# Between output and up projection: activation sums emitted ahead of the early products, weight splits strewn among them

## The chip, the cores and the metric

The kernel runs on one core of one Trainium2 chip. The metric is device time in microseconds (us) of one execution, the median of several runs. Five engines work side by side, each through its own list of instructions in order: TensorE (PE; its weight loads are listed as PEld), VectorE (DVE), ScalarE (ACT), GpSimd (POOL) and SyncE (SP, which issues nearly all transfers here). They meet through semaphores: an instruction waits until another engine has counted far enough, and everything behind it on its own engine waits with it.

## The reference, cut to what matters

An encoder block on 1024 tokens of width 1024, all in float32: a mixing sub-layer (latent attention and a matrix-memory branch, merged by gates), then an MLP with a squared ReLU, then a last norm. The change stands where the mixing sub-layer's output projection ends and the MLP begins:

```
merged = (jax.nn.sigmoid(gate_a) * (y_attn @ w_branch_mla[l])
          + jax.nn.sigmoid(gate_b) * (y_mlstm @ w_branch_mlstm[l]))
x = x + merged @ w_out[l]                                # output projection, 1024 x 1024
u = rmsnorm(x, norm_mlp_g[l]) @ w_mlp_up[l]              # up projection, 1024 x 4096
x = x + jnp.square(jax.nn.relu(u)) @ w_mlp_down[l]       # down projection, 4096 x 1024
```

The norm's factor per token is a positive number, so it goes through the squared ReLU as its square: the kernel leaves it out of the up projection and multiplies it in behind the down projection (`rsq`).

## The kernel before, in words

**Split numbers.** Every float32 operand of a matmul is split into a high part (`h`, rounded to the fp32r type by a cast on ACT, L79) and a low part (`l`, what the cast left, by a subtraction on DVE, L80). A product is then three matmuls: high by high, high by low, low by high. `split` is thus always ACT first, DVE second, and a product can start when the cast is done but needs the subtraction by its second or third matmul.

**Output projection** (the loop at L1193). Eight token tiles of 128 in two halves of four. Each tile takes 48 matmuls into a PSUM tile of two banks (`a`, two such tiles), then DVE adds the residual (L1202, `xm`), and SP stores the sum for the end of the kernel (L1204). Once a half is there, PE transposes it (L1215) into single-bank PSUM tiles (`b`, four of them, handed round) and ACT copies each with the norm's gain to SBUF (L1216, `xf`): four blocks for the half, `blk[K half, token half, i]`. For the first half they are split at once. ACT then takes the sums of squares of the four `xm` tiles (L1225, `msq`).

**Up projection.** It is worked by pairs of 128-column weight blocks, 16 pairs (`Pair`, `up_pair`). With K and the tokens cut in two halves each, a pair is a 2 x 2 by 2 x 2 block product, and it is done with seven block products in place of eight (Winograd's form of Strassen's method). So sums of blocks are needed beforehand:

- of the activations, once for all pairs: T1, T2, T3, T4 (differences of blocks, L1236, `xt`) and block 22, each two tiles of 128x1024, each split (`bh`, `bl`);
- of the weights, for each pair: `sums` (L1109 to L1123) makes S1 to S4 and block 22 with four DVE sums, three casts and three subtractions; `plain` (L1103) only splits the pair's first block.

A product is 4 slices of K by 3 matmuls: 12 matmuls of 128x512 (L1139). Two of the seven products (blocks 11 and 12 by activations of the first token half) need no sums. For the first five pairs (`EARLY`) they are done ahead, by `first_products`: 12 matmuls into a `b` bank, an ACT copy to `r` (L1149), 12 more matmuls into the same bank, a second ACT copy (L1151). The second 12 must wait for the first copy, since they add to the same bank.

**What sets the order.** The kernel's code is written in Python and recorded; a scheduler then lays out each engine's list, mostly in the order in which the code is written, with some exchange of neighbours. Tiles come from pools handed out in turn: 46 slots of 4 KB for nearly everything, four buffers (`wr`) for raw weights. Who takes a slot or a buffer waits until its earlier holder was last read. Before, the order was: both halves with their squares; five times `plain` and `first_products`; `sums` of pair 0; then all the differences and splits T2, T3, T1, T4, 22; then the pairs, each with the `sums` of the next pair ahead of it.

Of the kernel before, what the change touches and what calls it, by code (L numbers as in the profile page):

```python
# [10 lines left out]
F32 = mybir.dt.float32  # L11
F32R = mybir.dt.float32r
I32 = mybir.dt.int32
AF = mybir.ActivationFunctionType
ALU = mybir.AluOpType
# [3 lines left out]
P = 128  # L19
# [4 lines left out]
EPS = 1e-6  # L24
# [14 lines left out]
def kernel(ctx: ExitStack, tc: tile.TileContext, x, positions, norm_mix_g, w_in, mla_q_norm_g,  # L39
                      mla_w_uq, mla_kv_norm_g, mla_w_ukv, mlstm_conv_w, mlstm_conv_b, mlstm_igate_b,  # L40
                      mlstm_fgate_b, mlstm_out_norm_g, w_branch_mla, w_branch_mlstm, w_out, norm_mlp_g,
                      w_mlp_up, w_mlp_down, norm_final_g, out, dbg=None):
    nc = tc.nc
# [12 lines left out]
    def nm(p):  # L56
        cnt[0] += 1
        return f"{p}{cnt[0]}"

    def slot(shape, dt=F32, p="s"):  # L60
        return sl.tile(shape, dt, tag="s", name=nm(p))
# [4 lines left out]
    def bankA(p="a"):  # L66
        return psa.tile([P, 1024], F32, tag="A", name=nm(p))

    def bankB(p="b"):
        return psb.tile([P, 512], F32, tag="B", name=nm(p))  # L70

    def dump(name, ap, dst):
        if name in dbg:
            nc.sync.dma_start(out=dst(dbg[name]), in_=ap)


    def split(h, l, src, scale=None, eng=None):
        if scale is None:
            nc.scalar.copy(out=h, in_=src)  # L79
            (eng or nc.vector).tensor_tensor(out=l, in0=src, in1=h.bitcast(F32), op=ALU.subtract)  # L80
        else:
            nc.scalar.activation(out=h, in_=src, func=AF.Copy, scale=scale)
            nc.vector.scalar_tensor_tensor(out=l, in0=src, scalar=scale, in1=h.bitcast(F32),
                                           op0=ALU.mult, op1=ALU.subtract)
# [113 lines left out]
    def nat_mm(ps, tr, t, wts, extra=()):  # L198

        n = len(wts)  # L200
        for k in range(n):
            xh, xl = tr.tile(t, k)
            wh, wl = wts[k]
            nc.tensor.matmul(out=ps, lhsT=xh, rhs=wh, start=(k == 0), stop=False)  # L204
            nc.tensor.matmul(out=ps, lhsT=xh, rhs=wl, start=False, stop=False)  # L205
            nc.tensor.matmul(out=ps, lhsT=xl, rhs=wh, start=False, stop=(k == n - 1))  # L206
# [84 lines left out]
    for d in range(2):  # L291
        t = tri[d]
# [48 lines left out]
    def vec(n, i):  # L341
        return vecs[:, vo[n] + i:vo[n] + i + 1]
# [783 lines left out]
    pairs = [Pair(p) for p in range(NP)]  # L1126
    EARLY = 5
# [4 lines left out]
    def product(o, p, a, b, first):  # L1132

        ah, al = pairs[p].ops[a]
        for k in range(4):
            bh, bl = B[b][k // 2]
            bh, bl = bh[:, k % 2], bl[:, k % 2]
            for i, (x_, y_) in enumerate(((ah, bh), (ah, bl), (al, bh))):
                nc.tensor.matmul(out=o, lhsT=x_[:, k], rhs=y_, start=(first and k == 0 and i == 0),  # L1139
                                 stop=(k == 3 and i == 2), skip_group_check=True)  # L1140

    early = {}

    def first_products(p):

        b1 = bankB()
        r = slot([P, 2, 512], F32, "r")
        product(b1, p, "11", "11", True)
        nc.scalar.copy(out=r[:, 1], in_=b1)  # L1149
        product(b1, p, "12", "21", False)  # L1150
        nc.scalar.copy(out=r[:, 0], in_=b1)  # L1151
        return r
# [37 lines left out]
    msq = const.tile([P, 8], F32, name="msq")  # L1190
    rsq = const.tile([P, 8], F32, name="rsq")
    blk = {}
    for half in range(2):  # L1193
        xs = []
        for j in range(4):
            t = half * 4 + j
            xx = slot([P, 1024], F32, "xm")
            nc.sync.dma_start(out=xx, in_=x[0, t * P:(t + 1) * P, :])
            pa = bankA()
            for n in range(2):  # L1200
                nat_mm(pa[:, n * 512:(n + 1) * 512], mg, t, wo[n])
            nc.vector.tensor_tensor(out=xx, in0=pa, in1=xx, op=ALU.add)  # L1202
            dump("xmid", xx, lambda o, t=t: o[t])
            nc.sync.dma_start(out=xmd[t], in_=xx)  # L1204
            xs.append(xx)
        if half == 1:
            pairs[0].load(1)
            pairs[0].plain()
        for q in range(4):
            f = slot([P, 2, 512], F32, "xf")  # L1210
            for i in range(2):
                k = 2 * q + i
                pb = bankB()
                for j in range(4):
                    nc.tensor.transpose(out=pb[:, j * P:(j + 1) * P], in_=xs[j][:, k * P:(k + 1) * P], identity=ident)  # L1215
                nc.scalar.activation(out=f[:, i], in_=pb, func=AF.Copy, scale=vec("gmlp", k))  # L1216
            blk[q // 2, half, q % 2] = f
            if half == 0:
                h, l = slot([P, 2, 512], F32R, "bh"), slot([P, 2, 512], F32R, "bl")
                split(h, l, f)  # L1220
                B.setdefault(f"{q // 2 + 1}1", []).append((h, l))
        for j in range(4):
            t = half * 4 + j
            junk = slot([P, 1024], F32, "j")
            nc.scalar.activation(out=junk, in_=xs[j], func=AF.Square, scale=1.0 / 32.0, accum_out=msq[:, t:t + 1])  # L1225
    nc.vector.tensor_scalar(out=rsq, in0=msq, scalar1=EPS, scalar2=None, op0=ALU.add)
    nc.vector.reciprocal(out=rsq, in_=rsq)

    def parts(name, f):
        h, l = slot([P, 2, 512], F32R, "bh"), slot([P, 2, 512], F32R, "bl")  # L1230
        split(h, l, f)
        B.setdefault(name, []).append((h, l))

    def minus(a, b):
        o = slot([P, 2, 512], F32, "xt")
        nc.vector.tensor_tensor(out=o, in0=a, in1=b, op=ALU.subtract)  # L1236
        return o

    for p in range(EARLY):
        if p > 0:  # L1240
            pairs[p].load(1)
            pairs[p].plain()
        early[p] = first_products(p)
    pairs[0].load()
    pairs[0].sums()
    t1 = [minus(blk[0, 1, q], blk[0, 0, q]) for q in range(2)]
    t2 = [minus(blk[1, 1, q], t1[q]) for q in range(2)]
    for q in range(2):
        parts("T2", t2[q])
    for q in range(2):  # L1250
        parts("T3", minus(blk[1, 1, q], blk[0, 1, q]))
    for q in range(2):
        parts("T1", t1[q])
    for q in range(2):
        parts("T4", minus(blk[1, 0, q], t2[q]))
    for q in range(2):
        parts("22", blk[1, 1, q])


    for p in range(NP):  # L1260
# [102 lines left out]
```

## Time and profile before

| | us |
|---|---|
| median of 3 runs | 1719.27 (1718.85 to 1720.53) |
| the profiled execution, its own time | 1718.16 |
| its span, first to last instruction | 1716.5 |
| PE busy, share of the span | 1658.3, 97% |
| DVE, ACT, POOL busy | 927.4, 683.9, 188.2 |
| mean granted TensorE clock | 0.989 of full speed |

The span's times count from its first instruction; a time such as "at 1001.58" below is on that scale. The profile cuts the span in 40 slices of 42.9 us. In 36 of them PE is busy nine tenths or more; the first has 7 and the last 8 tenths, and two in the middle, slices 24 and 25, have 8 and 5: that is the stretch from 987 to 1073 us, between the output projection and the pairs. Slice 25 is also the only one in which the granted clock reads less than 9 tenths: 7. A PE matmul's time in the trace is 0.39 us, but at full clock one starts every 0.23 us; PE's busy time therefore says whether it has work, and the distance of starts says how fast it goes. ACT and DVE overlap the end of one instruction with the start of the next in the same way, by about 0.1 us.

### The profile page before, as it was taken

What the parts mean: (1) busy time and instruction counts of PE and PEld (TensorE: products, weight loads), DVE (VectorE), ACT (ScalarE), POOL (GpSimd) and SP (SyncE); (2) the same over time, 40 slices, a digit from 0 to 9 for tenths busy, and PEclk for the clock granted to TensorE, in tenths of its full rate; (3) what the DMA queues carried; (4) which work ended last, traced back from release to release, by engine and by line L of the source; (5) the groups of instructions that cost most, each with busy time, mean ns of one, the idle gap of its engine ahead of it and who ended that gap; (6) DMA issues with size and microseconds to landing.
All of it is one profiled execution on the core that took longest, in us unless ns stands there. A gap on an engine that the chain in (4) does not pass through costs nothing.

```text
span 1716.5 us, 21981 instructions
## 1 busy us (share of the span) xinstructions
PE 1658.3 (97%) x8613; PEld 1394.4 (81%) x8613; DVE 927.4 (54%) x1405; ACT 683.9 (40%) x1211; POOL 188.2 (11%) x363
## 2 busy tenths in 40 slices
PE   7999999999999999999999985999999999999998
PEld 6789989888879979898878863778888788888886
DVE  5676766632233386777873217655444564444324
ACT  6254443531122476766732333445443531111101
POOL 4112020100002434343200000000000000000001
PEclk9999999999999999999999997999999999999999
DMA  7112110113221000000165211443332673332002
GB/s 212 37 38 62 38 38 13 62 56 92 62 98 56 1 13 2 1 13 1 38 244 173 99 62 37 136 134 123 123 99 98 235 244 99 98 98 93 31 1 98
DMA packets 112651, 139.68 MB, mean 81 GB/s; under 512 B 5971, under 2 KB 88868, under 8 KB 112548
## 3 DMA queue, kind: packets, MB, share of 16 engines
q1 hardware_dynamic: 112516, 138.28, 24.8%
q8 instruction: 68, 1.11, 0.3%
q14 instruction: 35, 0.29, 0.1%
q10 hardware_dynamic: 32, 0.01, 0.0%
HBM read 104.71 MB, written 33.55 MB: 81 GB/s over the span
## 4 chain that ended last, share of the span: by engine, by line
PE 86%; issue 6%; DVE 3%; ACT 3%; POOL 1%; DMA 1%; SPq 0%; POOLq 0%; DVEq 0%; ACTq 0%
PE b L1139 18%; PE a L232 7%; PE a L227 7%; PE a L228 7%; PE b L1299 6%; PE b L1303 6%; PE b L1300 6%; PE a L204 4%; PE a L206 4%; PE a L205 4%; PE b L984 3%; PE av L1001 2%; PE av L1002 1%; PE a L963 1%; PE a L965 1%
## 5 line engine op out<-in xcount | busy, mean ns | idle before, releaser
L1299 PE MATMUL b<-wh,hh 128*128 128x512 f32 x512 | 201.0, 394 | 1.2 <-DVE xm L1309 1.2
L227 PE MATMUL a<-th,wh 128*128 128x512 f32 x504 | 202.0, 401 | 0.0
L228 PE MATMUL a<-tl,wh 128*128 128x512 f32 x504 | 201.8, 400 | 0.0
L1300 PE MATMUL b<-wl,hh 128*128 128x512 f32 x512 | 200.7, 393 | 0.0
L79 ACT CAST wh<-wr 128x1024 fp32r<-128x1024 f32 (+6 forms) x118 | 111.0, 961 | 191.2 <-PE b L1300 161.5
L1139 PE MATMUL b<-bh,wh 128*128 128x512 f32 x384 | 155.4, 406 | 24.9 <-ACT bh L79 11.1
L1309 DVE SCALAR_TENSOR_TENSOR xm<-b,rsq,xm 128x512 f32<-128x512 f32 x128 | 90.0, 746 | 155.6 <-PE b L1303 155.3
L232 PE MATMUL a<-th,wl 128*128 128x512 f32 x504 | 162.9, 400 | 0.0
L204 PE MATMUL a<-wh,th 128*128 128x256 f32 (+5 forms) x504 | 161.7, 322 | 0.2 <-ACT mo L569 0.2
L205 PE MATMUL a<-wl,th 128*128 128x256 f32 (+5 forms) x504 | 160.4, 319 | 0.1
L206 PE MATMUL a<-wh,tl 128*128 128x256 f32 (+5 forms) x504 | 160.5, 319 | 0.0
L1303 PE MATMUL b<-wh,hl 128*128 128x512 f32 x512 | 160.1, 393 | 0.0
L1139 PE MATMUL b<-bl,wh 128*128 128x512 f32 x384 | 154.5, 402 | 1.1 <-DVE bl L80 1.1
L1139 PE MATMUL b<-bh,wl 128*128 128x512 f32 x384 | 153.3, 402 | 0.0
L80 DVE TENSOR_TENSOR wl<-wr,wh 128x1024 fp32r<-128x1024 f32 (+6 forms) x118 | 131.3, 1128 | 35.4 <-ACT wh L79 34.8
L306 POOL TENSOR_SCALAR m<-m 128x1 f32<-128x1 f32 (+1 forms) x40 | 8.9, 223 | 1196.5 <-ACT o L1314 854.7
L1299 PEld LDWEIGHTS b<-wh,hh 128*128 128x128 f32 x512 | 96.1, 188 | 24.0 <-DVE xm L1309 1.6
L1303 PEld LDWEIGHTS b<-wh,hl 128*128 128x128 f32 x512 | 96.1, 188 | 22.3
L1300 PEld LDWEIGHTS b<-wl,hh 128*128 128x128 f32 x512 | 96.1, 188 | 22.2 <-DVE wl L80 0.2
L1139 PEld LDWEIGHTS b<-bh,wh 128*128 128x128 f32 x384 | 74.2, 193 | 46.7 <-ACT bh L79 12.0
L227 PEld LDWEIGHTS a<-th,wh 128*128 128x128 f32 x504 | 94.7, 188 | 21.1 <-issue 1.0
L228 PEld LDWEIGHTS a<-tl,wh 128*128 128x128 f32 x504 | 94.7, 188 | 20.7 <-issue 0.5
(287 smaller groups left out, 3331.2 us busy)
## 6 DMA issues: line engine op xcount, KB each, us to landing
wr<-in_w_mlp_up SPq DMA_DIRECT2D x37, 512.0 KB, 5.0
hid<-r SPq DMA_DIRECT2D x32, 512.0 KB, 2.6
u<-hid SPq DMA_DIRECT2D x32, 512.0 KB, 5.0
wr<-in_w_mlp_down SPq DMA_DIRECT2D x32, 512.0 KB
wr<-in_w_in SPq DMA_DIRECT2D x24, 512.0 KB, 3.7
x<-in_x SPq DMA_DIRECT2D x8, 512.0 KB, 5.9
da<-sg SPq DMA_DIRECT2D x8, 512.0 KB, 2.6
db<-sg SPq DMA_DIRECT2D x8, 512.0 KB, 2.6
```

What stands on the lines that cost most here:

```text
L79: nc.scalar.copy(out=h, in_=src)
L80: (eng or nc.vector).tensor_tensor(out=l, in0=src, in1=h.bitcast(F32), op=ALU.subtract)
L204: nc.tensor.matmul(out=ps, lhsT=xh, rhs=wh, start=(k == 0), stop=False)
L205: nc.tensor.matmul(out=ps, lhsT=xh, rhs=wl, start=False, stop=False)
L206: nc.tensor.matmul(out=ps, lhsT=xl, rhs=wh, start=False, stop=(k == n - 1))
L227: nc.tensor.matmul(out=o, lhsT=wts[k][0], rhs=xh, start=(k == 0), stop=False)
L228: nc.tensor.matmul(out=o, lhsT=wts[k][0], rhs=xl, start=False, stop=False)
L232: nc.tensor.matmul(out=o, lhsT=wts[k][1], rhs=xh, start=False, stop=(k == n - 1))
L1139: nc.tensor.matmul(out=o, lhsT=x_[:, k], rhs=y_, start=(first and k == 0 and i == 0), stop=(k == 3 and i == 2), skip_group_check=True)
L1299: nc.tensor.matmul(out=pos[n], lhsT=a[:, ts_], rhs=wh[:, c], start=(i == 0), stop=False)
L1300: nc.tensor.matmul(out=pos[n], lhsT=a[:, ts_], rhs=wl[:, c], start=False, stop=False)
L1303: nc.tensor.matmul(out=pos[n], lhsT=b[:, ts_], rhs=wh[:, c], start=False, stop=(i == FC - 1))
```

## The change

All of it is in the part between output and up projection. No instruction of the calculation is added or taken away; the code's order is another:

- the sums of squares of the second token half move from straight behind its transposes to the end of the part, behind the split of block 22, with `rsq`;
- `plain` of pairs 0 and 1 moves up between the output projection's tiles of the second half, behind tiles 1 and 3;
- the differences t1 and t2 and the split of T2 come first, with `plain` of pair 2 in between; then pair 0's two blocks are loaded, the early products of pairs 0 and 1 run, and the `sums` of pair 0;
- then T3, `plain` of pair 3 and the early products of pair 2; T1, `plain` of pair 4 and the early products of pair 3; T4 and the early products of pair 4; block 22.

```
+    def squares(half, xs):
+        for j in range(4):
+            t = half * 4 + j
+            junk = slot([P, 1024], F32, "j")
+            nc.scalar.activation(out=junk, in_=xs[j], func=AF.Square, scale=1.0 / 32.0, accum_out=msq[:, t:t + 1])
...
-        if half == 1:
-            pairs[0].load(1)
-            pairs[0].plain()
+            if half == 1 and j in (1, 3):
+                pairs[j // 2].load(1)
+                pairs[j // 2].plain()
...
+        if half == 0:
+            squares(half, xs)
...
-    for p in range(EARLY):
-        if p > 0:
-            pairs[p].load(1)
-            pairs[p].plain()
-        early[p] = first_products(p)
-    pairs[0].load()
-    pairs[0].sums()
+
     t1 = [minus(blk[0, 1, q], blk[0, 0, q]) for q in range(2)]
+    pairs[2].load(1)
+    pairs[2].plain()
     t2 = [minus(blk[1, 1, q], t1[q]) for q in range(2)]
     for q in range(2):
         parts("T2", t2[q])
+    pairs[0].load()
+    for p in range(2):
+        early[p] = first_products(p)
+    pairs[0].sums()
     for q in range(2):
         parts("T3", minus(blk[1, 1, q], blk[0, 1, q]))
+    pairs[3].load(1)
+    pairs[3].plain()
+    early[2] = first_products(2)
     for q in range(2):
         parts("T1", t1[q])
+    pairs[4].load(1)
+    pairs[4].plain()
+    early[3] = first_products(3)
     for q in range(2):
         parts("T4", minus(blk[1, 0, q], t2[q]))
+    early[4] = first_products(4)
     for q in range(2):
         parts("22", blk[1, 1, q])
+    squares(1, xs)
```

What the scheduler makes of it is seen in the engines' lists. First, ACT, straight behind the second half's last `xf`; before (`j` are the squares' scratch tiles, `r` the copies of the early products, `wh` casts of weights):

```order
L1225 ACTIVATE j_9667,msq<-xm_9397 128x1024
L1225 ACTIVATE j_9669,msq<-xm_9450 128x1024
L1225 ACTIVATE j_9671,msq<-xm_9503 128x1024
L1225 ACTIVATE j_9673,msq<-xm_9556 128x1024
L1149 COPY r_9678<-b_9677 128x512
L79 CAST wh_9707<-wr_9705 128x1024
L1151 COPY r_9678<-b_9677 128x512
L1149 COPY r_9712<-b_9711 128x512
L79 CAST wh_9741<-wr_9739 128x1024
L1151 COPY r_9712<-b_9711 128x512
```

And the same place of ACT's list now (`bh` from `xt` are casts of T2, `wh` and `w` from `ws` and `wr_9697` those of pair 0's sums; `b_9699` and `b_9727` are the banks of pairs 0 and 1):

```order
L79 CAST wh_9679<-wr_9677 128x1024
L79 CAST bh_9687<-xt_9683 128x1024
L79 CAST bh_9691<-xt_9685 128x1024
L1149 COPY r_9700<-b_9699 128x512
L1149 COPY r_9728<-b_9727 128x512
L79 CAST wh_9759<-ws_9755 128x1024
L1151 COPY r_9700<-b_9699 128x512
L79 CAST wh_9765<-ws_9756 128x1024
L1151 COPY r_9728<-b_9727 128x512
L79 CAST w_9769<-wr_9697 128x512
```

The squares are gone from here, and casts of activation and weight sums stand among the copies. Second, ACT at the third pair's first copy; before (early pairs 2 and 3):

```order
L1149 COPY r_9746<-b_9745 128x512
L79 CAST wh_9775<-wr_9773 128x1024
L1151 COPY r_9746<-b_9745 128x512
L1149 COPY r_9780<-b_9779 128x512
L79 CAST wh_9809<-wr_9807 128x1024
L1151 COPY r_9780<-b_9779 128x512
```

And now, where `r_9791` belongs to pair 2 (`b_9790`), `wh_9786` to pair 3, `wh_9828` to pair 4, and the four `bh` are T3 and T1:

```order
L79 CAST bh_9774<-xt_9772 128x1024
L79 CAST bh_9780<-xt_9778 128x1024
L79 CAST wh_9786<-wr_9784 128x1024
L1149 COPY r_9791<-b_9790 128x512
L79 CAST bh_9818<-xt_9673 128x1024
L79 CAST bh_9822<-xt_9675 128x1024
L79 CAST wh_9828<-wr_9826 128x1024
L1151 COPY r_9791<-b_9790 128x512
```

Pair 2's first copy now stands behind both casts of T3 and behind pair 3's cast. Third, PE in the middle of pair 2's early products; before (`b_9745` is pair 2's bank; the fourth row is the first matmul of its second product):

```order
L1139 MATMUL b_9745<-bh_9351,wh_9741 128x512
L1139 MATMUL b_9745<-bl_9352,wh_9741 128x512
L1139 MATMUL b_9745<-bh_9351,wl_9742 128x512
L1139 MATMUL b_9745<-bh_9368,wh_9741 128x512
L1139 MATMUL b_9745<-bl_9369,wh_9741 128x512
```

And now (`b_9727` pair 1, `b_9790` pair 2, `b_9832` pair 3; the third row ends pair 2's first product, the fifth begins its second):

```order
L1139 MATMUL b_9727<-bl_9386,wh_9617 128x512
L1139 MATMUL b_9727<-bh_9385,wl_9618 128x512
L1139 MATMUL b_9790<-bh_9351,wl_9680 128x512
L1139 MATMUL b_9832<-bh_9334,wh_9786 128x512
L1139 MATMUL b_9790<-bh_9368,wh_9679 128x512
```

Between the two products of one pair there are now matmuls of other pairs, and pair 3's first matmul has come ahead of pair 2's second product.

## Rows read from the trace of the kernel before

**Rows 1.** The page's busy time by engine over the whole span.

```profile
PE 1658.3 (97%) x8613; PEld 1394.4 (81%) x8613; DVE 927.4 (54%) x1405; ACT 683.9 (40%) x1211; POOL 188.2 (11%) x363
```

**Rows 2.** PE's waits, whole span: who waited for whom, us in all, times, longest.

```profile
PE b L1139 <- ACT bh L79: 11.1, 2, 8.0
PE b L1139 <- ACT wh L79: 7.7, 1, 7.7
PE b L1139 <- ACT r L1149: 6.0, 5, 3.3
...
PE b L1299 <- DVE xm L1309: 1.2, 1, 1.2
PE b L1139 <- DVE bl L80: 1.1, 2, 0.7
```

**Rows 3.** PE's timeline: start, duration, instruction, idle before it and its releaser.

```profile
1001.58 0.50 PE L1139 MATMUL b<-bh,wh 128*128 128x512 f32 x1
...
1007.94 0.80 PE L1139 MATMUL b<-bh,wh 128*128 128x512 f32 x1 [3.31 <-ACT r L1149]
...
1015.75 0.50 PE L1139 MATMUL b<-bh,wh 128*128 128x512 f32 x1 [0.68 <-ACT r L1149]
...
1046.36 0.79 PE L1139 MATMUL b<-bh,wh 128*128 128x512 f32 x1 [8.02 <-ACT bh L79]
...
1048.63 0.63 PE L1139 MATMUL b<-bh,wh 128*128 128x512 f32 x1
1049.06 0.63 PE L1139 MATMUL b<-bl,wh 128*128 128x512 f32 x1
...
1069.69 0.80 PE L1139 MATMUL b<-bh,wh 128*128 128x512 f32 x1 [7.75 <-ACT wh L79]
...
1075.39 0.53 PE L1139 MATMUL b<-bh,wh 128*128 128x512 f32 x1
```

**Rows 4.** Stretches: length, busy time (count) by engine, granted clock, DMA share, GB/s.

```profile
1001.58:1075.39 73.81, 47.76 (x158) 34.51 (x158) 37.56 (x39) 30.45 (x41) 0.00 (x0) 0.79 0.18 50
1016.10:1021.19 5.09, 5.09 (x24) 4.13 (x22) 1.23 (x1) 1.14 (x2) 0.00 (x0) 1.00 0.35 99
1048.21:1051.62 3.41, 3.41 (x9) 2.63 (x8) 2.30 (x3) 1.04 (x1) 0.00 (x0) 0.50 0.00 0
1075.39:1279.00 203.61, 203.61 (x877) 163.57 (x876) 113.84 (x152) 95.29 (x108) 0.00 (x0) 1.00 0.39 121
```

**Rows 5.** ACT's timeline from the second half's last activations on.

```profile
1003.10 1.11 ACT L1225 ACTIVATE j<-xm 128x1024 f32<-128x1024 f32 x1
...
1004.14 1.10 ACT L1225 ACTIVATE j<-xm 128x1024 f32<-128x1024 f32 x1
...
1038.37 0.59 ACT L1151 COPY r<-b 128x512 f32<-128x512 f32 x1 [2.18 <-PE b L1139]
1038.86 1.05 ACT L79 CAST wh<-ws 128x1024 fp32r<-128x1024 f32 x1
1039.80 0.62 ACT L79 CAST w<-wr 128x512 fp32r<-128x512 f32 x1
...
1049.87 1.04 ACT L79 CAST bh<-xt 128x1024 fp32r<-128x1024 f32 x1 [2.43 <-DVE xt L1236]
```

**Rows 6.** DVE's timeline through pair 0's sums and the first splits.

```profile
1036.22 1.23 DVE L80 TENSOR_TENSOR wl<-ws,wh 128x1024 fp32r<-128x1024 f32 x1 [3.97 <-ACT wh L79]
1037.36 0.68 DVE L1116 TENSOR_TENSOR ws<-wr,wr 128x512 f32<-128x512 f32 x1
1037.97 0.69 DVE L1117 TENSOR_TENSOR ws<-wr,ws 128x512 f32<-128x512 f32 x1
...
1048.62 1.22 DVE L1236 TENSOR_TENSOR xt<-xf,xf 128x1024 f32<-128x1024 f32 x1
1050.94 1.23 DVE L80 TENSOR_TENSOR bl<-xt,bh 128x1024 fp32r<-128x1024 f32 x1 [1.11 <-ACT bh L79]
```

**Rows 7.** Transfers issued from 960 to 1016 us: size, time from issue to landing.

```profile
wr<-in_w_mlp_up SPq DMA_DIRECT2D x2, 512.0 KB, 5.0
```

More of the change, by code (lines that the diff above doesn't have):

```diff
@@ L1221 @@
                 B.setdefault(f"{q // 2 + 1}1", []).append((h, l))
[L1222 to L1227, printed above, removed]
+        if half == 0:
+            squares(half, xs)
     def parts(name, f):
@@ L1249 @@
         parts("T2", t2[q])
+    pairs[0].load()
+    for p in range(2):
+        early[p] = first_products(p)
+    pairs[0].sums()
     for q in range(2):
         parts("T3", minus(blk[1, 1, q], blk[0, 1, q]))
+    pairs[3].load(1)
+    pairs[3].plain()
+    early[2] = first_products(2)
     for q in range(2):
         parts("T1", t1[q])
+    pairs[4].load(1)
+    pairs[4].plain()
+    early[3] = first_products(3)
     for q in range(2):
         parts("T4", minus(blk[1, 0, q], t2[q]))
+    early[4] = first_products(4)
     for q in range(2):
         parts("22", blk[1, 1, q])
+    squares(1, xs)
+    nc.vector.tensor_scalar(out=rsq, in0=msq, scalar1=EPS, scalar2=None, op0=ALU.add)
+    nc.vector.reciprocal(out=rsq, in_=rsq)
     for p in range(NP):
```

## The prediction

> **What bounds the kernel now.** I read the busy times first, then PE's waits, then PE's timeline around the longest of them, then counts and clock by stretch, and last what ACT and DVE do there. PE is busy in 97% of the span [rows 1], so only 58 us are without a matmul at all. PE's list of waits shows where a good part of them is: the up projection's line L1139 waits 11.1 us for casts of activations, 7.7 for a cast of weights, 6.0 for the copies of the early products and 1.1 for subtractions, 25.9 us in all [rows 2]. The timeline shows them one behind the other: 3.31, then 0.68 (four of that kind), 8.02, 3.1 (the second of the two that make 11.1) and 7.75 us [rows 2, 3]. From 1075.39 to 1279 PE is then busy without a break, 203.61 of 203.61 us [rows 4], and the one wait listed behind that is 1.2 us in the down projection [rows 2]. So the only stretch that can give much is 1001.58 to 1075.39.
>
> What is lost in it is more than the waits. By the code 156 matmuls start there: 120 of the five early pairs and three more products of 12 (the view counts 158 with those that overlap the edges). At full pace one matmul starts every 203.61 / 877 = 0.232 us [rows 4], so they need 36.2 us. They took 73.8. The loss is 37.6 us: 25.9 of waits, and 11.7 of slow running, mostly at the low clock: in 1048.21 to 1051.62 the granted clock is 0.50 of full, the level of 1.2 GHz [rows 4], and starts are 0.43 us apart (1048.63, 1049.06) [rows 3], 0.20 more than at full pace.
>
> The Trainium skill (Perfetto Trace Analysis, "Identifying the Most-Contended Engine") warns that the busy share of matmuls is not a good measure of how close PE is to its limit. The trace agrees: that stretch of 3.41 us reads wholly busy for only 9 matmuls [rows 4]. If busy time were the measure, this stretch would have 25.9 us to give and not 37.6; with the 11.1 us of new waits found below the gain would be 14.8 and the time near 1704, in place of 1695.
>
> The wait is for two engines that work by turns: a split is a cast on ACT and then a subtraction on DVE, and while one of them works on a tile the other often waits, as DVE 1.11 us for a cast [rows 6]. In this stretch DVE is busy 37.6 us and ACT 30.5 [rows 4]. Before, all the differences and their splits run when the early products are over, so PE has nothing left to do beside them.
>
> **The change part by part.** I number L1139's matmuls from the one at 1001.58. Up to there nothing that PE waits for changes: two weight casts and subtractions (1.05 and 1.23 us each [rows 5, 6]) now stand between the output projection's tiles, and DVE adds the second half's first residual some 2 us later, behind one of them; PE needs that PSUM tile only two tiles, about 11 us, later.
>
> *Squares away from the copies.* The four squares take ACT 1.04 us each from start to start (1003.10, 1004.14) [rows 5], 4.2 us ahead of pair 0's copy; the wait of 3.31 us goes with them. In their place stand pair 2's cast and the two casts of T2. DVE does pair 2's subtraction and the two t2 before the second of those can run: 1003.10 + 1.05 + 1.14 + 1.14 + 1.22 = 1007.7, the cast to 1008.7, the two copies (0.50 and 0.59) by 1009.8. PE comes to pair 0's second product as matmul 36, at 1001.58 + 35 x 0.232 = 1009.7, and needs only the first copy, ready at 1009.3. No wait, with 0.4 us to spare.
>
> *Two pairs by turns.* Between the two products of pair 0, and of pair 1, stand 23 or more matmuls of other pairs, 5 us and more. The waits of 0.68 us go there, and later ones too.
>
> *A new wait at pair 3.* PE's row is 12, 12 and 11 matmuls of pairs 0, 1, 2, then 12 and 12 (second products of 0 and 1), one of pair 2, and then matmul 61, pair 3's first. It comes up at 1001.58 + 60 x 0.232 = 1015.5. It needs pair 3's cast, and pair 2's second product needs pair 2's first copy, which stands behind that cast on ACT. What stands ahead of both is a chain of turns. Back to back a cast takes ACT 0.95 (1038.86 to 1039.80) and a subtraction takes DVE 1.14 (1036.22 to 1037.36), a half-size sum 0.61; an operation that the other engine waits for counts in full, 1.05, 1.23 or 0.69 [rows 5, 6]. From the end of the activations at 1003.10:
>
> - ACT pair 2's cast 1.05; DVE its subtraction, two t2, two T2 subtractions 5 x 1.14 = 5.70, first two sums 0.72 + 0.69
> - ACT cast 1.05; DVE subtraction, third and fourth sum 1.14 + 0.61 + 0.69
> - ACT cast 1.05; DVE subtraction, block 22's, first T3 difference 1.14 + 0.61 + 1.22
> - ACT first T3 cast 1.05; DVE its subtraction, second difference 1.14 + 1.22
> - ACT second T3 cast and pair 3's cast 0.95 + 1.05
>
> These are 21.1 us, and nine handovers at 0.03 us (a difference ends at 1048.62 + 1.22 = 1049.84, its cast begins at 1049.87 [rows 5, 6]) make 21.4: pair 3's cast ends at 1024.5. PE waits 9.0 us there. Matmul 62 wants the copy behind it and starts at 1025.0, 9.25 us late. All weights are in SBUF by then, since their loads were issued before 1006 and land in 5.0 us [rows 7].
>
> *The clock.* Behind the wait of 7.75 us the 12 matmuls that follow took from 1069.69 to 1075.39 [rows 3], 5.70 us in place of 2.78, with a short wait for a subtraction among them; behind the first wait of 0.68 us PE ran at 1.00 (1016.10 to 1021.19 [rows 4]). For 9 us I take 12 matmuls at 0.20: 2.4 us. From below it is nothing, from above two such spells, 5 us.
>
> *Smaller waits later.* Pair 4 and the second products up to matmul 144 find their casts done. Matmul 145 is the first with pair 1's sums. PE comes to it at 1025.0 + 83 x 0.232 + 2.4 = 1046.7. Its cast stands behind pair 4's copies, block 22's two casts and the squares. The copy goes at 1038.5, behind matmul 108. Then 0.50, two casts 1.9, 0.4 for a slot, a square 1.04, a copy 0.50, three squares 3.1, the cast 1.05: 1047.0, 0.4 late, and its subtraction 0.3 more. Here the moved squares cost: this chain goes with PE's own matmul 108, so an earlier PE gains nothing on it. Then DVE: matmul 169 adds to a bank whose last content DVE must first have read. That add is queued behind all of pair 1's subtractions and sums and is done at 1053.05, 0.1 late. Matmul 181 follows 169 to 180 without anything between and waits for the next add, 0.9. Together 1.7 us.
>
> *Hidden.* On SP the loads stand in another order among the stores, and each still waits until DVE is done with one of the four raw buffers. Pair 4's load, behind the last store and pair 2's subtraction, is issued at about 1005, lands at 1010 and is needed at 1027. Pair 1's second load is issued at about 1018, lands at 1023 and is needed at 1042. If that cover were gone, a load would cost its 5.0 us. The factor `rsq` comes 38 us later than before and is first needed in the down projection.
>
> *Sum.* New loss 9.25 + 2.4 + 1.7 = 13.4 us against 37.6: 24 us gained. From the pairs on PE has no break in either order, so all of it stays. The profiled execution's 1718.16 less 24.2 is 1694; the runs' median is 1.1 above that execution, which gives 1695.
>
> **The rivals.**
>
> *The clock lingers.* The low level comes back behind the waits around matmuls 145 to 181 and lasts longer behind the first, so that 5 us are paid in place of 2.4, the small waits double, and a second spell of 12 matmuls costs 2.4 more: 24.2 - 2.6 - 1.7 - 2.4 = 17.5 us gained, about 1702. For it: the low spells in the trace follow waits, and 1.7 us in small ones are new. Against: the 0.68 us waits did nothing to the clock. The Trainium skill (TensorE: Matmul & The Clock Gate, "A second HAM failure mode") tells of kernels whose short idles between groups of matmuls make the clock fall again and again; the stretch with the 0.68 us waits, at 1.00 throughout, does not bear that out.
>
> *Nothing is saved.* DVE and ACT have the same work as before and may keep their turns just as long, so that PE's loss is only laid elsewhere: 1719. Against it: they begin the sums at 999, not at 1031, and 37.6 us of DVE with its handovers fit before 1053.
>
> *Slower.* The wait of 9 us sets the clock low at matmul 61 and the engine stays low through pairs 0 and 1, as it was low again and again from 1041 to 1075. Each matmul then costs 0.20 more; 24.2 + 2.4 us are used up by 133 of them, that is at matmul 194. Low up to pair 1's end (matmul 240) it is 36 us, 9.4 more than the point of balance: 1729. Against: from 62 to 144 nothing interrupts PE, and before it was back at full pace at 1075.39, 12 matmuls behind the wait of 7.75 us [rows 3, 4].
>
> **How the numbers follow.** The forecast 0.83, the lingering clock 0.10, nothing saved 0.04, slower 0.03. The likeliest is 1695. Its own range: a chain that is 1.5 us shorter and no low clock, 1691; two spells and a chain 1.5 us longer, 1699. The lingering clock reaches to 1702, so 1690 to 1702. A measurement of this kernel tells from no change what is over 0.2%, 3.4 us: faster 0.93 (the first two), within 0.04, slower 0.03.
>
> **What would show it.** In PE's waits: 3.3 and the 0.68s for `r` gone, the two for `bh` gone, one of about 9 us for a weight cast, at about 1015 to 1024, with matmul 61 behind it; two or three below 1 us between 1046 and 1057; nothing later. ACT's squares at about 1042 to 1046. Matmul 157 at about 1050 in place of 1075. It is wrong if there is a second wait of more than 2 us, if the clock is low beyond some 15 matmuls behind the first, or if a later stage shows a wait of its own that takes the gain back.

## The result, and the profile after

The changed kernel takes 1693.9 us (median of 4 runs, 1693.44 to 1694.64) against 1719.17 (1718.85 to 1720.53) beside it: a ratio of 0.9852, interval 0.9835 to 0.9869. Forecast were 1695.0, range 1690 to 1702. The profiled execution took 1694.64, its span is 1692.9.

The page's busy times, which answer to [rows 1]: every engine has as many instructions as before. PE's share rises by a point because the span is shorter. Its busy time falls by 6.8 us without any work less: fewer of its matmuls run at the low clock.

```profile
PE 1651.5 (98%) x8613; PEld 1391.0 (82%) x8613; DVE 927.9 (55%) x1405; ACT 684.2 (40%) x1211; POOL 188.5 (11%) x363
```

PE's waits of line L1139 in the changed kernel (releaser, us in all, times, longest), against [rows 2]: 25.9 us have become 10.0. No wait for an `r` or a `bh` is left.

```profile
PE b L1139 <- ACT wh L79: 9.2, 2, 8.8
PE b L1139 <- DVE u L1161: 0.8, 1, 0.8
```

PE's timeline, against [rows 3]. The rows are matmuls 1, 61 and 62 together, 63, 70, 71, 145, 149, 157, 169 and 181 of the up projection, counted as in the prediction.

```profile
1001.95 0.50 PE L1139 MATMUL b<-bh,wh 128*128 128x512 f32 x1
...
1024.94 1.28 PE L1139 MATMUL b<-bh,wh 128*128 128x512 f32 x2 [8.85 <-ACT wh L79]
1026.02 0.63 PE L1139 MATMUL b<-bl,wh 128*128 128x512 f32 x1
...
1028.97 0.40 PE L1139 MATMUL b<-bh,wl 128*128 128x512 f32 x1
1029.21 0.40 PE L1139 MATMUL b<-bh,wh 128*128 128x512 f32 x1
...
1046.88 0.50 PE L1139 MATMUL b<-bh,wh 128*128 128x512 f32 x1 [0.36 <-ACT wh L79]
...
1048.14 0.50 PE L1139 MATMUL b<-bh,wl 128*128 128x512 f32 x1
...
1050.08 0.39 PE L1139 MATMUL b<-bl,wh 128*128 128x512 f32 x1
...
1052.93 0.50 PE L1139 MATMUL b<-bh,wh 128*128 128x512 f32 x1
...
1056.76 0.50 PE L1139 MATMUL b<-bh,w 128*128 128x512 f32 x1 [0.78 <-DVE u L1161]
```

Matmul 157 comes 48.13 us behind matmul 1; before it was 73.81. A wait shorter than a matmul's 0.39 us hardly shows as idle time; it is read from the distance of starts. Matmul 149 starts 0.46 behind its forerunner and 169 starts 0.30 behind, where 0.23 is the pace.

The stretches, against [rows 4] (length, busy time and count of PE, PEld, DVE, ACT, POOL, granted clock, DMA share, GB/s): matmul 1 to 157, the long wait, the nine starts behind it, and what follows.

```profile
1001.95:1050.08 48.13, 38.86 (x158) 30.39 (x157) 32.65 (x34) 28.32 (x39) 0.00 (x0) 0.89 0.20 55
1016.09:1024.94 8.85, 0.01 (x1) 0.00 (x0) 6.29 (x6) 4.40 (x7) 0.00 (x0) 0.65 0.42 118
1024.94:1028.97 4.03, 4.03 (x9) 3.10 (x10) 4.01 (x5) 3.28 (x4) 0.00 (x0) 0.51 0.30 84
1050.08:1254.00 203.92, 203.14 (x873) 162.61 (x872) 115.04 (x154) 95.37 (x109) 0.00 (x0) 1.00 0.40 122
```

The clock falls within the wait and is at its low level for nine starts behind it: 4.03 us in place of 9 x 0.232 = 2.09. From matmul 157 on PE goes at the pace of before: 203.92 / 873 = 0.234.

ACT's timeline, against [rows 5]: the first T2 casts, pair 0's first copies, the two T3 casts with pair 3's cast and pair 2's copy behind them, and the first and last of the moved squares.

```profile
1007.00 2.19 ACT L79 CAST bh<-xt 128x1024 fp32r<-128x1024 f32 x2 [2.43 <-DVE xt L1238]
1009.09 1.07 ACT L1149 COPY r<-b 128x512 f32<-128x512 f32 x2
...
1019.43 1.05 ACT L79 CAST bh<-xt 128x1024 fp32r<-128x1024 f32 x1 [2.02 <-DVE xt L1238]
1022.90 1.05 ACT L79 CAST bh<-xt 128x1024 fp32r<-128x1024 f32 x1 [2.42 <-DVE xt L1238]
1023.85 1.04 ACT L79 CAST wh<-wr 128x1024 fp32r<-128x1024 f32 x1
1024.80 0.58 ACT L1149 COPY r<-b 128x512 f32<-128x512 f32 x1
...
1041.12 1.06 ACT L1198 ACTIVATE j<-xm 128x1024 f32<-128x1024 f32 x1 [0.34 <-DVE bl L80]
...
1044.75 1.05 ACT L1198 ACTIVATE j<-xm 128x1024 f32<-128x1024 f32 x1
```

DVE's timeline of the same time, against [rows 6]: the two T3 differences and their subtractions.

```profile
1018.18 1.22 DVE L1238 TENSOR_TENSOR xt<-xf,xf 128x1024 f32<-128x1024 f32 x1
1020.51 1.23 DVE L80 TENSOR_TENSOR bl<-xt,bh 128x1024 fp32r<-128x1024 f32 x1 [1.11 <-ACT bh L79]
1021.65 1.22 DVE L1238 TENSOR_TENSOR xt<-xf,xf 128x1024 f32<-128x1024 f32 x1
```

ACT idles 2.02 and 2.42 us ahead of the two T3 casts, DVE 1.11 ahead of the subtraction: each waits for the other's turn while PE waits for the last cast. That is the chain.

### The profile page after: what moved, and what is told of

The parts are those of the page before. It is cut to its first block, busy times and chain, and to the rows that moved or that the text cites. A ratio compares the mean times of both kernels' runs of the same rounds, so it can differ in the third digit from the quotient of the medians.

```text
span 1692.9 us, 21982 instructions
## 1 busy us (share of the span) xinstructions
PE 1651.5 (98%) x8613; PEld 1391.0 (82%) x8613; DVE 927.9 (55%) x1405; ACT 684.2 (40%) x1211; POOL 188.5 (11%) x363
## 3 DMA queue, kind: packets, MB, share of 16 engines
q8 instruction: 68, 1.11, 0.3%
## 5 line engine op out<-in xcount | busy, mean ns | idle before, releaser
L1139 PE MATMUL b<-bh,wh 128*128 128x512 f32 x384 | 152.1, 398 | 9.2 <-ACT wh L79 9.2
L1139 PE MATMUL b<-bl,wh 128*128 128x512 f32 x384 | 151.7, 395 | 0.0
L1139 PE MATMUL b<-bh,wl 128*128 128x512 f32 x384 | 150.7, 395 | 0.1
L80 DVE TENSOR_TENSOR wl<-wr,wh 128x1024 fp32r<-128x1024 f32 (+6 forms) x118 | 131.3, 1128 | 23.5 <-ACT wh L79 19.0
L232 PEld LDWEIGHTS a<-th,wl 128*128 128x128 f32 x504 | 94.0, 188 | 21.2 <-issue 0.2
```

The lines of the kernel that those rows point to most:

```text
L232: nc.tensor.matmul(out=o, lhsT=wts[k][1], rhs=xh, start=False, stop=(k == n - 1))
```

## The experiments

Theory: PE's loss is the length of the chain that ACT and DVE go through by turns, seen at the points where PE comes to its ends; the change saves what it lays beside matmuls. Rival: the gain comes from the two simple parts alone (squares out of the way, two pairs by turns), and strewing the splits matters little. A second question is what the wait that is left costs, by itself and by the clock.

The first early product starts anywhere from 1000.7 to 1003.0 in the executions below, in no order with the kernels. Part of that goes with something far ahead of the change: the three latest (1001.95 in the changed kernel, 1002.98 in e3, 1002.20 in e4) are the three with a granted clock of 0.89 from 505 to 520 us, where the others have 1.00. So beside the time I give the stretch from matmul 1 to the span's end, of the profiled execution. Where two kernels' medians lie 1 or 2 us apart, that stretch carries the comparison. It is one execution for each kernel; the two of the changed kernel differ by 0.4 us in it.

| | time, us | ratio to before (interval) | matmul 1 to end | waits of L1139 |
|---|---|---|---|---|
| before | 1718.0 to 1719.2 (medians) | | 714.92 | 25.9 |
| changed | 1693.90 | 0.9852 (0.9835–0.9869) | 690.95 | 10.0 |
| changed, again | 1694.81 | 0.9864 (0.9849–0.9879) | 690.57 | 10.0 |
| e1 squares alone | 1715.50 | 0.9987 (0.9978–0.9996) | 712.64 | 24.5 |
| e3 turns alone | 1714.69 | 0.9981 (0.9972–0.9990) | 710.12 | 22.4 |
| e5 both of these | 1711.57 | 0.9961 (0.9949–0.9974) | 708.77 | 22.1 |
| e2 changed, squares back | 1695.99 | 0.9875 (0.9861–0.9888) | 692.71 | 10.8 |
| e4 changed, pair 2 ahead | 1692.71 | 0.9854 (0.9841–0.9868) | 688.00 | 5.8 |
| e6 changed, wait filled | 1692.65 | 0.9849 (0.9835–0.9862) | 689.35 | 2.6 |
| e8 another order | 1690.04 | 0.9835 (0.9821–0.9848) | 686.64 | 5.6 |
| e9 GpSimd takes three | 1692.82 | 0.9848 (0.9834–0.9861) | 689.64 | 8.9 |
| e10 another order, GpSimd takes three | 1689.60 | 0.9827 (0.9814–0.9841) | 687.66 | 6.0 |

The changed kernel was run again beside e5, e6 and e8:

> The changed kernel as it is, once more beside the next three on one chip. All theories: about 25 us less than the kernel before.

It shows the same three waits, 8.85, 0.36 and 0.78, and the same gain: 714.92 - 690.57 = 24.35 us, 23.97 in the first profile.

**e1, the squares alone.** The kernel before, with the second half's squares and `rsq` behind the split of block 22.

```
-        for j in range(4): ... (squares)
+        if half == 0:
+            squares(half, xs)
...
         parts("22", blk[1, 1, q])
+    squares(1, xs)
```

> The kernel before with one part of the change: the second half's squares (and rsq) stand behind the split of block 22. Theory (the gain of 25.3 us is mostly the laying of the differences and splits beside the early products; the squares are a small part): PE's wait of 3.31 us for pair 0's copy falls to 0.7 and the low clock behind it goes, but the squares now stand ahead of pair 1's first sum cast, whose wait grows by about 1 us; 4 us less than before, about 1715. Rival (ACT's queue ahead of the copies is the cause, so the squares carry most of the gain): more than half of 25.3, below 1706.

PE's timeline, the wait at the first copy, at the first T2 cast and at pair 1's weight cast:

```profile
1004.88 0.50 PE L1139 MATMUL b<-bh,wh 128*128 128x512 f32 x1 [0.67 <-ACT r L1149]
...
1042.01 0.79 PE L1139 MATMUL b<-bh,wh 128*128 128x512 f32 x1 [8.02 <-ACT bh L79]
...
1066.46 0.80 PE L1139 MATMUL b<-bh,wh 128*128 128x512 f32 x1 [8.86 <-ACT wh L79]
```

The first wait falls from 3.31 to 0.67, and at 1042.01 the kernel is ahead of before by 44.78 - 40.85 = 3.93 us, both counted from matmul 1. At 1066.46 it is ahead by 2.81, at the end by 2.28. The wait for the weight cast has grown from 7.75 to 8.86. So the squares are worth 3.9 us where they stood, and the next end of the chain takes 1.1 of that back; 0.5 more goes behind it and was not traced further. The theory had 4 us for the whole; it came out at 2.3, and 2.5 by the medians. The rival, with more than half of 25.3, falls.

**e3, two pairs by turns alone.** The kernel before, with each pair's second product written behind the next pair's first.

```
-        early[p] = first_products(p)
+            nexth = first_half(p)
+        early[p - 1] = second_half(p - 1, *held)
+        held = nexth
```

> The kernel before with one part of the change: the early products taken by turns (first product of pair p + 1 ahead of the second product of pair p); differences, splits and squares stand where they stood. Theory: the four waits of 0.68 us go, the wait of 3.31 us stays, pair 0's sums start a little earlier; 5 us less than before, about 1714. Rival (the turns carry most of the gain): below 1706.

PE's waits of this line, as in [rows 2]:

```profile
PE b L1139 <- ACT bh L79: 9.2, 2, 6.5
PE b L1139 <- ACT wh L79: 8.5, 1, 8.5
PE b L1139 <- ACT r L1148: 3.3, 1, 3.3
```

4.8 us gained from matmul 1 to the end, 3.3 by the medians; 5 were expected, and the rival falls. All four waits of about 0.68 are gone; the first, 3.31, stays, since the squares still stand ahead of the copy, and the long waits stay, at 6.46, 2.76 and 8.50.

**e5, both of these.** The two edits together, the differences and splits left in one block behind the early products.

> The kernel before with both small parts of the change, the squares at the end and the early products by turns, but with differences and splits where they stood. Theory (laying the differences and splits beside the early products is the main part): 5 to 7 us less than the kernel before, PE's waits of about 8, 3 and 9 us behind the early products all stay; the other 18 to 20 of the 25.3 us belong to the laying. Rival (the small parts only fail alone and give the gain together): below 1700.

PE's timeline, the waits over 1 us:

```profile
1038.81 0.80 PE L1139 MATMUL b<-bh,wh 128*128 128x512 f32 x1 [8.02 <-ACT bh L79]
...
1047.89 0.80 PE L1139 MATMUL b<-bh,wh 128*128 128x512 f32 x1 [3.31 <-ACT bh L79]
...
1063.26 0.80 PE L1139 MATMUL b<-bh,wh 128*128 128x512 f32 x1 [8.97 <-ACT wh L79]
```

6.15 us gained, 6.8 by the medians, and all the long waits of [rows 3] are still there: 8.02, 3.31 and 8.97 where they were 8.02, 3.1 and 7.75. The other 18 us of the 24 belong to what this kernel lacks: the T sums, their splits and pair 0's sums beside early products, and the weight splits moved up. How the 18 divide among these no run separates. The rival falls.

**e2, the changed kernel with its squares back.** Behind the second half's transposes, as before.

```
-        if half == 0:
-            squares(half, xs)
+        squares(half, xs)
...
-    squares(1, xs)
```

> The changed kernel with the second half's squares put back straight behind its transposes. Theory: three small waits appear at the start (about 1.3, 0.8 and 1.6 us, for pair 2's cast and pair 0's copy), the wait at matmul 61 grows by about 1 us, the small waits near matmul 145 to 149 go: 2.5 us slower than the changed kernel, about 1696.5. Rival (squares carry most): most of the gain is gone, above 1706.

PE's timeline up to the long wait, and the clock in a stretch behind the first two (columns as above):

```profile
1007.90 0.50 PE L1139 MATMUL b<-bh,wh 128*128 128x512 f32 x1 [0.98 <-ACT wh L79]
1009.16 0.50 PE L1139 MATMUL b<-bh,wl 128*128 128x512 f32 x1 [0.53 <-DVE wl L80]
...
1028.32 1.28 PE L1139 MATMUL b<-bh,wh 128*128 128x512 f32 x2 [9.33 <-ACT wh L79]
```

```profile
1010.00:1013.00 3.00, 3.00 (x8) 1.93 (x7) 3.00 (x5) 2.64 (x4) 0.00 (x0) 0.50 0.67 175
```

1.8 to 2.1 us lost against the changed kernel, where 2.5 were expected; the rival falls. Two waits appear at the start and not three: the squares no longer stop a copy, but pair 2's cast behind them is late for its first product; the waits are 0.98 and 0.53, the clock is at half for a while, and the long wait ends 27.2 us behind matmul 1 in place of 23.0. The waits of 0.36 and 0.78 near matmuls 145 and 181 are gone here, which gives part of it back: matmul 157 is 4.0 us later than in the changed kernel, matmul 193 only 2.9.

**e4, pair 2 ahead.** The early products of pair 2 written ahead of T3 and of pair 3's split.

```
     pairs[0].sums()
+    early[2] = first_products(2)
     ... (T3, pair 3's load and split)
-    early[2] = first_products(2)
```

> The changed kernel with the early products of pair 2 written ahead of T3 and of pair 3's split. Theory (the wait of 8.85 us at matmul 61 is one of ACT's order: pair 2's copy stands behind T3's casts): the wait splits into about 2.2 us for pair 2's copy at matmul 61 and 4.3 for pair 3's cast at matmul 73, 2.8 us of matmuls move into it; 2.7 us faster than the changed kernel, about 1691. Rival (the wait is the sum of DVE's and ACT's work up to there, whatever the order): waits of 9 us in all and the same time, 1694.

PE's timeline, the two waits in place of the one of 8.85:

```profile
1018.18 0.50 PE L1139 MATMUL b<-bh,wh 128*128 128x512 f32 x1 [1.82 <-ACT r L1149]
...
1025.35 0.68 PE L1139 MATMUL b<-bh,wh 128*128 128x512 f32 x1 [2.56 <-ACT wh L79]
```

2.6 to 3.0 us gained against the changed kernel. The chain to pair 3's cast is as long as it was (the cast ends 23.1 us behind matmul 1), but PE now works through pair 2's 12 second matmuls in that time, and loses 4.4 us in waits instead of 8.85. Part of that goes to slow running behind two waits in place of one: matmul 157 comes 45.61 us behind matmul 1 in place of 48.13. So the rival's 9 us of waits are not there. The whole times tell it less well: 1692.71 lies 25.3 us below the kernel before that ran beside it, and the changed kernel 25.3 and 23.5 below its own.

**e6, the long wait filled.** The changed kernel with 30 matmuls behind pair 0's sums that write to a PSUM tile nobody reads (`warm`): they add work and take none away. PE then waits 1.42 us more.

```
     pairs[0].sums()
+    warm = bankA("warm")
+    wa, _ = pairs[0].ops["S3"]
+    wb = B["11"][0][0]
+    for i in range(30):
+        nc.tensor.matmul(out=warm[:, 0:512], lhsT=wa[:, i % 4], rhs=wb[:, i % 2], start=True, stop=True)
```

> The changed kernel with 30 more matmuls of 128x512, whose result is not used, written behind pair 0's sums; they need pair 0's third sum cast and so stand in the wait of 8.85 us at matmul 61, 7 us of the 9. Theory (part of that wait's price is the low clock behind it): the wait shrinks to 1.5 to 2 us, the clock stays at its upper level and the time falls by about 2 us against the changed kernel, in spite of 7 us more work. Rival (the low clock costs nothing here because ACT and DVE are late anyway): same time as the changed kernel. Rival (PE's own work is the limit): 7 us slower.

PE's timeline, the filling and pair 3's first matmul, and the clock in two stretches of it:

```profile
1015.55 7.08 PE L1256 MATMUL warm<-bh,wh 128*128 128x512 f32 x30 [0.35 <-ACT wh L79]
...
1024.05 0.51 PE L1139 MATMUL b<-bh,wh 128*128 128x512 f32 x1 [1.42 <-ACT wh L79]
```

```profile
1015.55:1022.60 7.05, 7.05 (x30) 5.55 (x30) 5.31 (x5) 2.60 (x4) 0.00 (x0) 1.00 0.52 148
1024.05:1028.00 3.95, 3.95 (x17) 3.15 (x18) 3.93 (x5) 3.65 (x5) 0.00 (x0) 1.00 0.30 80
```

Pair 3's first matmul starts 23.00 us behind matmul 1 as in the changed kernel (22.99): the chain does not care what PE does. But the clock is at full, and 17 matmuls go where the changed kernel got 9 through in about the same time. The stretch to the end is 1.2 to 1.6 us shorter in spite of 7 us more of matmuls, the median 2.2 us lower than the changed kernel's on the same chip (1692.65 against 1694.81). That is the price of the clock behind this wait, shown by itself. Both rivals fall.

**e8, another order.** Pair 3's split and the T3 differences ahead of the early products; then pair 0's sums, pair 2's products, T3's splits, pair 4's split, pair 3's products, T1, the T4 differences, pair 4's products, T4's splits, block 22, the squares.

```
+    pairs[3].load(1)
+    pairs[3].plain()
     for p in range(2):
         early[p] = first_products(p)
+    t3 = [minus(blk[1, 1, q], blk[0, 1, q]) for q in range(2)]
     pairs[0].sums()
     ...
```

> The changed kernel with another order, meant to shorten what it still loses: pair 3's split and the early products of pairs 0 and 1, the T3 differences, pair 0's sums, pair 2's early products, T3's splits, pair 4's split, pair 3's early products, T1's splits, T4's differences, pair 4's early products, T4, block 22, squares. Theory (what is lost behind the change is the order in which ACT gets its casts): the wait of 8.85 us becomes one of 2.3 us at matmul 73 and one of about 3 us at matmul 145; 4 to 5 us faster than the changed kernel. Rival (the loss is ACT's and DVE's total work): same time.

PE's timeline, its two waits over 1 us:

```profile
1020.36 0.50 PE L1139 MATMUL b<-bh,wh 128*128 128x512 f32 x1 [1.96 <-ACT r L1149]
...
1041.93 0.80 PE L1139 MATMUL b<-bh,wh 128*128 128x512 f32 x1 [2.79 <-ACT wh L79]
```

3.9 to 4.3 us better than the changed kernel, 4.8 by the medians; the waits were expected at 2.3 and 3 us. The work of ACT and DVE is the same in another order, so the rival falls. It is faster than both kernels: 1688.63 to 1691.86 against 1694.03 to 1696.03 for the changed one beside it.

**e9, GpSimd takes three subtractions.** The changed kernel, with the low parts of the first blocks of pairs 2, 3 and 4 computed on GpSimd, which is idle in the stretch.

```
-            split(h, l, a)
+            split(h, l, a, eng=nc.gpsimd if self.p in (2, 3, 4) else None)
```

> The changed kernel, with the subtractions of the first-block splits of pairs 2, 3 and 4 on GpSimd in place of VectorE (three instructions of 128x1024; nothing left out). GpSimd is idle in this stretch. Theory (the wait of 8.85 us is the length of the turns that ACT and DVE take, and each subtraction on DVE is a term of it): pair 2's subtraction, 1.14 us, leaves the chain to pair 3's cast, so that wait is about 7.7 us, the clock's cost stays, the span from the first early product to the end falls from 690.6-690.95 by 1 to 2 us, the time is about 1693. The subtraction on GpSimd may take more than 2 us; PE needs it only behind 24 and more matmuls, so that costs nothing. Rival (GpSimd beside DVE slows DVE, or GpSimd is so slow that PE waits for a low part): DVE's instructions beside it take longer than 1.14 us from start to start, or PE shows a wait for a subtraction at L80, and the time is the same as the changed kernel's or up to 3 us longer.

The first two of GpSimd's subtractions, and DVE's at the same times:

```profile
1003.96 2.50 POOL L80 TENSOR_TENSOR wl<-wr,wh 128x1024 fp32r<-128x1024 f32 x1 [153.68 <-ACT wh L79]
...
1023.20 2.50 POOL L80 TENSOR_TENSOR wl<-wr,wh 128x1024 fp32r<-128x1024 f32 x1 [16.74 <-ACT wh L79]
```

```profile
1004.85 2.69 DVE L80 TENSOR_TENSOR bl<-xt,bh 128x1024 fp32r<-128x1024 f32 x1 [0.66 <-ACT bh L79]
...
1024.59 2.20 DVE L80 TENSOR_TENSOR bl<-xt,bh 128x1024 fp32r<-128x1024 f32 x1 [1.15 <-ACT bh L79]
```

Both were partly right. The wait falls from 8.85 to 7.74 and 0.9 to 1.3 us are gained to the end, the low side of what the theory gave. But DVE's subtraction beside GpSimd's takes 2.69 in place of 1.23, and it ends 1004.85 + 2.69 = 1007.54, 1.08 behind GpSimd's end at 1006.46: 1.46 us of what was taken off DVE come back as waiting.

That the wait fell by almost the 1.14 us of one subtraction is luck. In the changed kernel DVE does it like this, ahead of the two T2 subtractions:

```profile
1004.60 1.23 DVE L80 TENSOR_TENSOR wl<-wr,wh 128x1024 fp32r<-128x1024 f32 x1 [2.03 <-ACT wh L79]
1005.74 2.36 DVE L1238 TENSOR_TENSOR xt<-xf,xt 128x1024 f32<-128x1024 f32 x2
1008.08 2.36 DVE L80 TENSOR_TENSOR bl<-xt,bh 128x1024 fp32r<-128x1024 f32 x2
```

The T2 subtractions start 1008.08 - 1001.95 = 6.13 us behind matmul 1 here and 1004.85 - 1001.26 = 3.59 in e9: DVE no longer waits 2.03 for pair 2's cast either. That is 2.54 us, and less the 1.46 it is 1.08, about what the wait lost.

**e10, another order and GpSimd.** An order much like e8's, with pair 4's split ahead of pair 2's products and the T3 differences ahead of those of pairs 0 and 1, and e9's edit.

> A version of my own: the changed kernel with its parts in another order (pair 3's split and the T3 differences ahead of the early products of pairs 0 and 1; then pair 0's sums, pair 4's split, pair 2's early products, T3's splits, pair 3's, T1, the T4 differences, pair 4's, T4's splits, block 22, squares), and the three subtractions of pairs 2, 3 and 4 on GpSimd; nothing left out. Theory (what is left of the loss is the turns of ACT and DVE, and it is divided by laying each split where PE is busy with another pair): the reordering alone ran 686.6 us from the first early product to the end; without three subtractions of 1.14 us on DVE, two of them on the chain that PE waits for, 682 to 685, the time about 1685 to 1688. Rival (the reordered version is already at what the transfers and the clock allow): 686 to 688, time about 1690.

The rival's number came: 687.66 from matmul 1 to the end, against 686.64 in e8, and the medians are the same (1689.6, 1690.04). Its reason, transfers and clock, is not shown: PE's two long waits here, 2.9 and 2.3 us, are for casts. DVE's timeline shows one place where the gain went:

```profile
1004.33 6.04 DVE L80 TENSOR_TENSOR bl<-xt,bh 128x1024 fp32r<-128x1024 f32 x2 [0.66 <-ACT bh L79]
```

Two subtractions that take 2.36 together when GpSimd is idle take 6.04 beside two of GpSimd's, 3.7 us more; two subtractions of 1.14 less on DVE are 2.3. As e10 differs from e8 in order too, how much of its missing gain is this is not separated.

## Why the prediction was right

- **What is to gain.** 37.6 us were said to be lost ahead of matmul 157, and all but 13.4 to be saved. The new loss: 48.13 - 36.2 = 11.9 up to matmul 157, with 0.07 and 0.95 at 169 and 181 and 0.1 behind each of them, 13.1. From matmul 1 to the first matmul of the down projection it is 349.7 before and 325.5 now, 24.2 us gained, for which 24.2 stood in the sum; what differs later is 0.3 us and less. The medians differ by 25.3 in the first comparison and by 23.5 in the second. The distance of starts was the right measure and busy time was not: PE's waits fell by 25.9 - 10.0 = 15.9 us only, the other 8 are mostly matmuls that no longer run slowly. (The 11.1 us of new waits that the prediction sets against busy time should be 9.25 + 1.7 = 10.95; nothing hangs on it.) That the sum came so close is luck in part: the clock was put 0.5 too dear, and the small waits some 0.4 too cheap.
- **Squares away from the copies** and **two pairs by turns**: no wait for `r` is left. Their parts are 2.3 (e1), 4.8 (e3) and 6.15 together (e5); e1 shows that the first is worth 3.9 locally.
- **A new wait at pair 3**: predicted 9.0, measured 8.85. Pair 3's cast was to end 1024.5 - 1001.58 = 22.9 behind matmul 1; it does at 1023.85 + 1.04 - 1001.95 = 22.94. It holds on the way too: the first T3 difference ends 1018.18 + 1.22 - 1001.95 = 17.45 behind matmul 1 and the second 20.92, where the list of turns with its handovers gives about 17.4 and 20.8. Adding the two engines' turns, back to back where one runs on and in full where it waits, carried this.
- **The clock**: predicted 12 slow matmuls and 2.4 us; nine starts cost 4.03 - 2.09 = 1.9, and e6, which takes the slow running away, gains 1.2 to 2.2. Slightly too dear.
- **Smaller waits later**: predicted 0.4, 0.3, 0.1 and 0.9 at matmuls 145, 149, 169 and 181; the starts there are 0.53, 0.23, 0.07 and 0.95 late. All four were where they were said to be. What was left out is the 0.1 below.
- **Hidden**: no wait for a transfer and none for `rsq` appears.
- **The rivals.** The lingering clock: the low spell ended at 1028.97 and did not come back at the small waits. Nothing saved and slower fall with the result, and e8 shows that the order counts and not only the work of ACT and DVE. But the argument against the first rival, that waits of 0.68 do nothing to the clock, was too broad: in e2 two of 0.98 and 0.53 within 1.3 us were followed by a stretch at half.

## What to carry to other kernels

Where a result needs two engines in turn, add the turns one by one (back to back where the engine has work, in full where the other waits) and compare the end with the time at which the consumer comes up: the difference is the wait, and it was right to 0.15 us here. Moving an obstacle is worth what the next end of the same chain does not take back, and three quarters of this gain (18 of 24 us) came from strewing the chain beside other work. A wait of several us costs its low clock as well. Work of another group put there shortens the wait (e4), but it does not always save the clock: with 1.42 us of waiting left it stayed at full (e6), behind 1.82 and 2.56 it fell (e4).

## What the runs showed of the hardware that I had not expected

**DVE and GpSimd by turns.** A DVE subtraction with both inputs in SBUF that meets one of GpSimd's does not run beside it but ends about 1.08 us behind its end (1007.54 against 1006.46 and 1026.79 against 1025.70 in e9), which is nearly DVE's own 1.14. The Trainium skill (SBUF — State Buffer, "SBUF: two separate sides") says that the two engines share a pair of ports, given to one as an exclusive lock for a whole instruction, also where DVE has two SBUF inputs and the GpSimd instruction reads SBUF. These rows agree with it. GpSimd itself takes 2.50 us for what DVE does in 1.23.

**A fresh start costs 0.1.** Behind each short wait the second matmul starts 0.34 behind the first and not 0.23, at full clock (1046.88 and 1047.22, 1056.76 and 1057.10 in the changed kernel). So I count about 0.1 us for a wait beyond its length, even where the clock stays. The cause is not shown: single steps of 0.34 stand in the trace before as well, at matmuls 181, 237, 293 and 349, with no wait listed there.

**When the clock falls.** Waits of 0.67 to 0.73 spaced 6.5 us left it at full, four in the kernel before and five in e1; one of 0.36 and one of 0.78 did too (changed). It was at half behind 0.98 and 0.53 close together (e2), behind 1.96 and 2.79 (e8) and behind 8.85. Filled with 30 matmuls, the same stretch stayed at full. The wait of 1.42 that is left there had full clock behind it. So the length of a single wait does not tell it: 1.42 did nothing, and 0.98 with a second one close behind it did. The stretches (columns as above) behind the first wait of 0.67 in e1, then behind the two in e8:

```profile
1004.88:1037.00 32.12, 26.36 (x108) 19.89 (x108) 10.03 (x11) 11.43 (x16) 0.00 (x0) 1.00 0.27 77
```

```profile
1021.10:1024.40 3.30, 3.30 (x9) 2.53 (x9) 3.17 (x4) 2.05 (x3) 0.00 (x0) 0.50 0.67 196
1041.93:1044.90 2.97, 2.97 (x7) 2.39 (x8) 2.41 (x3) 0.48 (x1) 0.00 (x0) 0.50 0.02 6
```
